# Conformer module of a decoder trunk: convolution taps on TensorE and VectorE, whole projections, a lag of two tiles

## The chip, the cores and the metric

The kernel runs on one core of one Trainium2 chip. A core has five engines with an instruction queue each: TensorE (PE, matrix products; the loading of weights is shown apart as PEld), VectorE (DVE), ScalarE (ACT), GpSimd (POOL) and SyncE (SP, which here issues most DMAs). Each works through its queue in order and waits on semaphores for the others. The metric is the device time of one execution in microseconds (us). Three runs of the kernel before took 1326.22, 1327.00 and 1327.53 us, median 1327.0.

## What is computed

The program is two layers of a decoder over 512 tokens of 1024 channels: a mixed state-space and attention layer, a gated MLP, a Conformer convolution module, a second gated MLP. The change touches the Conformer alone:

```python
def conformer_conv_module(h, pw1_w, pw1_b, dw_w, dw_b, ln_w, ln_b, pw2_w, pw2_b):
    u = h @ pw1_w + pw1_b                                    # 512 x 2048
    u = u[..., :CONV_CH] * jax.nn.sigmoid(u[..., CONV_CH:])  # gate, 512 x 1024
    u = causal_depthwise_conv(u, dw_w, dw_b)                 # 31 taps per channel
    u = jax.nn.silu(layer_norm(u, ln_w, ln_b))               # over the 1024 channels
    return u @ pw2_w + pw2_b
```

`h` is the RMS-normalised residual stream, and the result is added to that stream.

## The kernel before

Activations lie with channels on the 128 partitions and the 512 tokens along the free dimension, so the 1024 channels are eight tiles, 0 to 7. A product in full precision is made of three TensorE passes: each weight block of 128x1024 is split into a rounded high half (`wh`, a copy on ScalarE, line 862) and the rest (`wl`, a subtraction, line 866, on VectorE for blocks 0 to 15, on GpSimd from 16 on), and `gemm` (lines 136 to 138) multiplies high by high, high by low and low by high. Blocks 0 to 15 are the first projection, two for each tile (value and gate); blocks 16 to 23 are the last one.

For each tile the code does this, in an order written out by hand (`tc.manual_schedule`), which is each engine's order:

- `project`: two products into PSUM banks `mm` (three of them). VectorE scales them by the token norm (`scaled`, line 222, and line 942), ScalarE takes the sigmoid (line 944), VectorE writes the gated tile into `u` (line 946), which has 30 zero columns in front.
- The convolution needs 31 shifted products. TensorE takes taps in groups of four: `u` goes to DRAM (`du`, line 956) and comes back in four shifted copies (line 959, tile tag `u4`), so that the 128 partitions hold 32 channels times 4 taps. A group is four matmuls of 128x32 weights, one for each quarter of the channels (line 885), into a bank `pa` (two of them). The weights are diagonal blocks that `make_diag` builds (line 842, GpSimd).
- `CONV` divides the taps: tiles 0 to 5 have four groups (16 taps) on TensorE, seven taps as products on ScalarE (line 917) added by GpSimd (line 918), eight on VectorE as multiply-adds (line 903); the first of these takes the TensorE result in `pa` as its addend, for tiles 1 to 4. Tiles 6 and 7 have seven groups on TensorE and three taps on VectorE, all of it in halves of 256 tokens, and so are their projections and gates.
- `merge` adds GpSimd's part, `sums` keeps running sums over tiles of the values and their squares, for the layer norm. From tile 2 on a matmul with `neg` subtracts a token mean that was estimated from tile 0 (line 891).

At the end, for each half of the tokens: `tail_sums` (line 995, TensorE), `moments` (lines 1000 to 1006 with `rsqrt`, sixteen small VectorE instructions), `spread` (line 1012, TensorE), then for each tile `normalise` (lines 1017, 1018 on VectorE, 1020, 1023 on ScalarE), `residue` (line 1028, VectorE) and `outputs` (lines 1035 to 1037, twelve matmuls for the first four output tiles). The other four output tiles are whole products behind that.

A tile's work is spread over two turns of the loop: in turn j, blocks 2j and 2j+1 are projected, GpSimd convolves tile j−1, VectorE tile j−2, and TensorE tile j−1 at the end of the turn.

Of the kernel before, what the change touches and what calls it, by code (L numbers as in the profile page):

```python
# [52 lines left out]
CONV = [(4, 7)] * 6 + [(7, 0), (7, 0)]  # L53
H = T // 2
U4 = 284
FILL = 2
SPR = 6
# [3 lines left out]
def kernel(ctx: ExitStack, tc: tile.TileContext, x, w_in, w_dt, w_out,  # L61
# [33 lines left out]
    def pload(group, pool, queue=nc.scalar):  # L95
        a, b = PGROUP[group]
        ptiles[group] = pool.tile([P, b - a], F32, name=f"par_{group}")
        queue.dma_start(ptiles[group], par[:, a:b])
# [713 lines left out]
    def conformer(norm, nxt):  # L812
        ops = norm.ops
        pad, width = 30, 30 + T + 2
        blk = lambda c: slice(c * P, (c + 1) * P)
        stack = con("stack")
        quad = lambda c: slice(32 * c, 32 * c + 32)
        s1 = sbt("s1", 1)
        s2 = sbt("s2s", 1)
        krows = phase[0].tile([64, T], F32R, name="krows")  # L820
        neg = phase[0].tile([64, P], F32R, name="neg")
        negf = sbt("cv", 2)[0:64, 0:P]
# [4 lines left out]
        dup = sbt("xh", 1, shape=[P, NB, 64])  # L827
        G.memset(dup, 0.0)
        ubuf = [phase[0].tile([P, width], F32, name=f"u{i}") for i in range(4)]
        for u in ubuf:  # L830
            G.memset(u[:, 0:pad], 0.0)
            G.memset(u[:, pad + T :], 0.0)
        w = lambda j, k: prm("dww", j * 31 + k)
        win = lambda j, k: ubuf[j % 3][:, k : k + T]
        half = lambda q: slice(H * q, H * q + H)
        u4, cvp, y, yp, raws, halves, diag = {}, {}, {}, {}, {}, {}, {}

        def make_diag(j):
            n = CONV[j][0]
            t = (sbt("dg", 6) if j < 6 else sbt("dl", 2, 1024))[:, : n * P]  # L840
            t = t.rearrange("p (g c m) -> p g c m", c=4, m=32)
            G.tensor_tensor(t.rearrange("p g c m -> p (g c) m"), stack.unsqueeze(1).to_broadcast([P, 4 * n, 32]),
                            prm("dw4", j * 32, 4 * n).unsqueeze(2).to_broadcast([P, 4 * n, 32]), op=ALU.mult)
            diag[j] = t

        def taps(j):
            npe, npl = CONV[j]
            k0 = min(4 * npe, 31)
            return range(k0, k0 + npl), range(k0 + npl, 31)
# [5 lines left out]
        def split_hi(i):  # L855
            if i in (20, 21):
                t = sbt("u4", 2, 8 * U4, F32R)
                halves[i] = t[:, :RING], t[:, RING : 2 * RING]
            else:
                a, b, n = ("xh", "xl", 1) if i in (15, 19) else ("wh", "wl", 3)  # L860
                halves[i] = sbt(a, n, RING, F32R), sbt(b, n, RING, F32R)
            S.copy(halves[i][0], raws[i])  # L862

        def split_lo(i):
            wh, wl = halves[i]
            (V if i < 16 else G).tensor_tensor(wl, raws.pop(i), f32(wh), op=ALU.subtract)  # L866
            if i + 3 < 24:
                load(i + 3)

        def project(i, q=None):  # L870
            bank = bank_of("mm")
            if q is None:
                gemm(bank, halves.pop(i), ops, True, True)
            else:
                gemm(bank[:, :H], halves[i], [(a[:, half(q)], b[:, half(q)]) for a, b in ops], True, True)
            return bank

        def conv_pe(j, q=None):
            n, k0 = (T, 0) if q is None else (H, q)
            npe = CONV[j][0]  # L880
            cv = cvp[j, q] = bank_of("pa")
            for g in range(npe):
                for c in range(4):
                    src = u4[j][:, c] if q is None else u4[j][:, q, c]
                    TE.matmul(cv[quad(c), :n], diag[j][:, g, c, :], src[:, 4 * g : 4 * g + n],  # L885
                              start=g == 0, stop=g == npe - 1 and j < 2)
            if j == 2:
                shift[0] = bank_of("pb")
                TE.matmul(shift[0], neg, krows, start=True, stop=True)
            if j > 1:  # L890
                TE.matmul(cv[:, :n], neg, krows if q is None else krows[:, half(q)], start=False, stop=True)

        def conv_dve(j, part):
            ks = list(taps(j)[1])
            if part == 0:
                y[j] = sbt("g", 16)
            n = len(ks)
            a, b = (4 * n + 5) // 11, (8 * n + 5) // 11
            for k in (ks[:a], ks[a:b], ks[b:])[part]:
                if j in (0, 5) and k == ks[0]:  # L900
                    V.tensor_scalar(y[j], win(j, k), w(j, k), None, op0=ALU.mult)
                    continue
                V.scalar_tensor_tensor(y[j], win(j, k), w(j, k), cvp[j, None] if k == ks[0] else y[j],  # L903
                                       op0=ALU.mult, op1=ALU.add)

        def conv_pool(j, part):
            ks = list(taps(j)[0])
            n = len(ks)
            if part == 0:
                yp[j] = sbt("yp", 2)  # L910
            a, b = (2 * n + 3) // 7, (5 * n + 3) // 7
            for k in (ks[:a], ks[a:b], ks[b:])[part]:
                if k == ks[0]:
                    S.activation(yp[j], win(j, k), AF.Identity, scale=w(j, k), bias=prm("dwb", j))
                    continue
                pr = sbt("pr", 2)
# [402 lines left out]
```

## Time and profile before

| | us |
|---|---|
| median of three runs | 1327.0 |
| the profiled execution, its own time | 1328.7 |
| its span, first to last instruction | 1326.9 |
| TensorE busy | 1288.5 |
| VectorE busy | 884.8 |
| GpSimd busy | 226.8 |

The Conformer's first matmul starts 742.5 us into the span, its last one ends near 958.9. "Busy" counts an instruction from its start to its end; matmuls overlap, so TensorE's busy share says little of how fast it works, and the granted clock (PEclk, 1.00 is full) is read beside it. A wait is idle time ahead of an instruction, put down to what ended it. Readings of the profile give line numbers of the kernel before.

### The profile page before, as it was taken

To read this page: it belongs to the slowest core of one execution; us is meant where nothing else is said; L and a number is where in the kernel's file an instruction comes from. 1 tells how busy PE (TensorE), PEld (TensorE's weight loads), DVE (VectorE), ACT (ScalarE), POOL (GpSimd) and SP (SyncE) were. 2 spreads that over 40 slices of the span, in tenths; PEclk is the share of its full clock that TensorE was granted. 3 is DMA by queue.
4 is the path that set the end of the run, shared out by engine and by line. 5 is a ranking of instruction groups with operands and counts; after the bars stand their busy time and mean duration, and the time that the engine had idled before them with its cause. 6 is when DMAs were issued, how large, how long until landed. Compare 5 with 4: busy or idle time off the path is not lost.

```text
span 1326.9 us, 17068 instructions
## 1 busy us (share of the span) xinstructions
PE 1288.5 (97%) x6480; PEld 1037.3 (78%) x6480; DVE 884.8 (67%) x1442; ACT 541.0 (41%) x855; POOL 226.8 (17%) x264
## 2 busy tenths in 40 slices
PE   8999999999999999999999999778999999999998
PEld 6878877778888888888888866557888888888887
DVE  7986769984368777777323378897667777774221
ACT  5465547853244333333223343325533333332120
POOL 0032205630210000000001186662500000000000
PEclk9999999989999999999999999789999999999999
DMA  6311222112232333333332373532233333333331
GB/s 219 96 49 64 65 80 62 52 48 80 96 98 95 96 95 98 99 103 91 88 102 90 96 185 106 141 93 71 83 95 96 95 96 98 100 98 97 108 112 38
DMA packets 41554, 125.19 MB, mean 94 GB/s; under 512 B 4864, under 2 KB 7808, under 8 KB 41472
## 3 DMA queue, kind: packets, MB, share of 16 engines
q1 hardware_dynamic: 40752, 123.56, 30.4%
q8 instruction: 51, 0.84, 0.3%
q10 hardware_dynamic: 720, 0.55, 0.2%
q14 instruction: 31, 0.25, 0.1%
HBM read 119.73 MB, written 4.35 MB: 94 GB/s over the span
## 4 chain that ended last, share of the span: by engine, by line
PE 69%; DVE 8%; POOL 2%; issue 1%; ACT 1%; POOLq 0%; ACTq 0%; DVEq 0%
PE mm L136 21%; PE mm L137 21%; PE mm L138 21%; DVE g L903 3%; POOL yp L918 1%; DVE wl L866 1%; DVE g L976 1%; PE pa L885 1%; PE pc L696 1%; PE pa L137 1%; PE pa L138 1%; PE pa L136 1%; PE pb L687 0%; POOL g L922 0%; PE mm L1036 0%
## 5 line engine op out<-in xcount | busy, mean ns | idle before, releaser
L136 PE MATMUL mm<-xr,wh 128*128 128x512 f32 (+1 forms) x1136 | 442.0, 389 | 1.0 <-ACT wh L862 1.0
L138 PE MATMUL mm<-xr,wl 128*128 128x512 f32 (+1 forms) x1136 | 439.8, 387 | 2.7 <-DVE wl L866 2.7
L137 PE MATMUL mm<-xr,wh 128*128 128x512 f32 (+1 forms) x1136 | 439.7, 387 | 0.0
L120 ACT CAST wh<-wr 128x1024 fp32r<-128x1024 f32 (+1 forms) x178 | 183.6, 1032 | 463.8 <-PE mm L137 420.2
L121 DVE TENSOR_TENSOR wl<-wr,wh 128x1024 fp32r<-128x1024 f32 (+1 forms) x178 | 214.2, 1204 | 162.9 <-ACT wh L120 157.5
L136 PEld LDWEIGHTS mm<-xr,wh 128*128 128x128 f32 x1136 | 214.6, 189 | 45.9 <-issue 2.8
L138 PEld LDWEIGHTS mm<-xr,wl 128*128 128x128 f32 x1136 | 214.8, 189 | 45.3 <-DVE wl L866 2.9
L137 PEld LDWEIGHTS mm<-xr,wh 128*128 128x128 f32 x1136 | 214.7, 189 | 41.7 <-DVE xr L184 0.4
L137 PE MATMUL mm<-g,wh 128*128 128x512 f32 x368 | 145.0, 394 | 0.0
L222 DVE TENSOR_TENSOR cv<-mm,nrb 128x512 f32<-128x512 f32 x114 | 78.2, 689 | 95.3 <-PE mm L138 90.5
L138 PE MATMUL mm<-g,wl 128*128 128x512 f32 x352 | 138.7, 394 | 0.0
L136 PE MATMUL mm<-g,wh 128*128 128x512 f32 x352 | 138.7, 394 | 0.0
L217 DVE SCALAR_TENSOR_TENSOR ct<-cv,par_ffn,ct 128x510 f32<-128x510 f32 (+1 forms) x176 | 131.0, 747 | 3.5 <-issue 0.4
L194 POOL TENSOR_TENSOR nsum<-nsum,nsq 128x512 f32<-128x512 f32 x21 | 33.8, 1611 | 433.1 <-ACT nsq L193 433.1
L137 PEld LDWEIGHTS mm<-g,wh 128*128 128x128 f32 x368 | 68.8, 187 | 17.1
L138 PEld LDWEIGHTS mm<-g,wl 128*128 128x128 f32 x352 | 65.8, 187 | 16.3
L136 PEld LDWEIGHTS mm<-g,wh 128*128 128x128 f32 x352 | 65.8, 187 | 16.3
L214 ACT ACTIVATE ct<-cv,par_ffn 128x512 f32<-128x512 f32 x88 | 71.4, 814 | 3.2 <-DVE cv L222 3.0
L918 POOL TENSOR_TENSOR yp<-yp,pr 128x512 f32<-128x512 f32 x36 | 59.9, 1663 | 37.4 <-ACT pr L917 35.8
L795 ACT ACTIVATE th<-ct 128x512 f32<-128x512 f32 x44 | 27.8, 632 | 84.5 <-DVE ct L217 84.4
L903 DVE SCALAR_TENSOR_TENSOR g<-u,par_conf,g 128x512 f32<-128x512 f32 x42 | 56.1, 1336 | 1.1
L806 DVE TENSOR_TENSOR h<-h,mm 128x512 f32<-128x512 f32 x16 | 11.0, 688 | 59.1 <-PE mm L138 59.1
(350 smaller groups left out, 1511.8 us busy)
## 6 DMA issues: line engine op xcount, KB each, us to landing
wr<-w_up SPq DMA_DIRECT2D x88, 512.0 KB, 3.5
wr<-w_in SPq DMA_DIRECT2D x29, 512.0 KB, 3.5
wr<-w_dn SPq DMA_DIRECT2D x32, 448.0 KB, 3.3
wr<-pw SPq DMA_DIRECT2D x24, 512.0 KB, 3.6
wr<-w_out SPq DMA_DIRECT2D x16, 512.0 KB, 3.6
wr<-w_dn SPq DMA_DIRECT2D x16, 512.0 KB, 3.5
u<-du SPq DMA_DIRECT2D x24, 262.0 KB, 4.7
u<-du SPq DMA_DIRECT2D x16, 140.0 KB, 2.9
```

The costliest lines, as they stand in the source:

```text
L120: S.copy(wh[:, :n], raw[:, :n])
L121: V.tensor_tensor(wl[:, :n], raw[:, :n], f32(wh[:, :n]), op=ALU.subtract)
L136: TE.matmul(bank, wh[:, c], xh, start=first and i == 0, stop=False)
L137: TE.matmul(bank, wh[:, c], xl, start=False, stop=False)
L138: end = TE.matmul(bank, wl[:, c], xh, start=False, stop=last and i == n - 1)
L194: eng.tensor_tensor(self.sum, self.sum, sq, op=ALU.add)
L214: S.activation(t, v, AF.Identity, bias=bias, scale=w(taps - 1))
L217: V.scalar_tensor_tensor(t[:, s:], v[:, : T - s], w(k), t[:, s:], op0=ALU.mult, op1=ALU.add)
L222: V.tensor_tensor(v, bank, rb, op=ALU.mult)
L795: S.activation(sg, c, AF.Silu)
L903: V.scalar_tensor_tensor(y[j], win(j, k), w(j, k), cvp[j, None] if k == ks[0] else y[j], op0=ALU.mult, op1=ALU.add)
L918: G.tensor_tensor(yp[j], yp[j], pr, op=ALU.add)
```

## The change

The Conformer's function is written anew; nothing else in the program changes but the size of its parameter tile.

- Taps: `GROUPS_PE = [6] * 7 + [8]`. Tiles 0 to 6 have six groups (24 taps) on TensorE and the other seven on VectorE (`taps`); tile 7 has eight groups (32 taps, one of them zero) on TensorE, in two halves. GpSimd and ScalarE do no taps.
- `make_diag` is on VectorE, one tile in each turn. The windows `u4` have three buffers instead of two, `du` takes only the columns that are needed.
- All projections are whole. TensorE's convolution of tile j−2 stands in turn j between its two projections, VectorE's taps of tile j−1 in two parts, and TensorE's result is added once (`add`).
- `sums` are on VectorE for all tiles. Weight blocks 16 to 19 are split on VectorE. Blocks 20 to 22 are split behind the second half's normalisations.
- The sums, moments and spreads of the two halves stand close together at the end, the second moments between tiles 2 and 3 of the first half's normalisations.

```diff
-CONV = [(4, 7)] * 6 + [(7, 0), (7, 0)]
+GROUPS_PE = [6] * 7 + [8]
...
+        def make_diag(j):
+            n = GROUPS_PE[j]
+            t = sbt("dg", 4, RING)[:, : n * P].rearrange("p (g c m) -> p g c m", c=4, m=32)
+            V.tensor_tensor(t.rearrange("p g c m -> p (g c) m"), stack.unsqueeze(1).to_broadcast([P, 4 * n, 32]),
+                            prm("dw4", j * 32, 4 * n).unsqueeze(2).to_broadcast([P, 4 * n, 32]), op=ALU.mult)
+            diag[j] = t
...
+        def conv_pe(j, q=None, part=None):
+            n, t0 = (T, 0) if q is None else (H, H * q)
+            npe = GROUPS_PE[j]
+            if part in (None, 0):
+                cvp[j, q] = bank_of("pa")
+            cv = cvp[j, q]
+            gs = range(npe) if part is None else range(npe // 2 * part, npe // 2 * (part + 1))
+            for g in gs:
+                for c in range(4):
+                    TE.matmul(cv[quad(c), :n], diag[j][:, g, c, :], u4[j][:, c, 4 * g + t0 : 4 * g + t0 + n],
                               start=g == 0, stop=g == npe - 1 and j < 2)
...
+        def taps(j, part):
+            ks = list(range(4 * GROUPS_PE[j], 31))
             if part == 0:
                 y[j] = sbt("g", 16)
+            m = (len(ks) + 1) // 2
+            for k in (ks[:m], ks[m:])[part]:
                 if k == ks[0]:
+                    V.tensor_scalar(y[j], win(j, k), w(j, k), prm("dwb", j), op0=ALU.mult, op1=ALU.add)
+                else:
+                    V.scalar_tensor_tensor(y[j], win(j, k), w(j, k), y[j], op0=ALU.mult, op1=ALU.add)
+
+        def add(j):
+            V.tensor_tensor(y[j], cvp.pop((j, None)), y[j], op=ALU.add)
...
+        def evacuate(q):
             if q == 0:
+                y[7], sq[7] = sbt("g", 16), sbt("nsq", 1)
+            for dst, fn in ((y[7], AF.Identity), (sq[7], AF.Square)):
+                S.activation(dst[:, half(q)], cvp[7, q][:, :H], fn, bias=prm("dwb", 7))
...
+            for j in range(7):
                 pa = project(2 * j)
                 if j == 0:
                     norm.reduce()
+                split_w(2 * j + 2)
+                make_diag(j)
                 if j >= 1:
+                    taps(j - 1, 0)
                 if j > 0:
                     va = scaled(pa, norm.rb)
+                if j >= 2:
+                    conv_pe(j - 2)
+                if j == 3:
+                    shift_mean()
                 pg = project(2 * j + 1)
...
+                split_w(2 * j + 3)
                 if j >= 1:
+                    taps(j - 1, 1)
                 if j >= 2:
+                    add(j - 2)
...
+                if j >= 4:
+                    sums(j - 2)
                 gate(j, va, pg)
+            pa = project(14)
+            make_diag(7)
+            split_w(16)
+            taps(6, 0)
+            va = scaled(pa, norm.rb)
+            pg = project(15)
+            split_w(17)
+            taps(6, 1)
+            gate(7, va, pg)
             conv_pe(5)
+            split_w(18)
+            add(5)
             sums(5)
+            conv_pe(6)
+            split_w(19)
+            add(6)
+            sums(6)
+            conv_pe(7, 0, 0)
+            conv_pe(7, 0, 1)
+            evacuate(0)
+            conv_pe(7, 1, 0)
             bank = tail_sums(0)
             lr = moments(bank)
+            conv_pe(7, 1, 1)
+            evacuate(1)
...
+            sa = spread(lr)
+            bank = tail_sums(1)
...
             normalise(0, 0, sa)
+            for j in range(1, 8):
                 normalise(j, 0, sa)
                 residue(j - 1, 0)
+                if j == 2:
+                    lr = moments(bank)
+            residue(7, 0)
+            for j in range(8):
                 outputs(j, 0)
+                if j == 4:
+                    sa = spread(lr)
             for j in range(8):
+                normalise(j, 1, sa)
                 if j:
                     residue(j - 1, 1)
             residue(7, 1)
+            for i in (20, 21, 22):
+                split_w(i)
             for j in range(8):
                 outputs(j, 1)
+            split_w(23)
```

In the rows below, as the built programs hold them, a row is line, operation, output and inputs by the program's names, output shape; `x3` marks equal rows in a run. VectorE before, one turn of the loop (turn 4: `g` is a tile's convolution, `u` the gated tiles, `pa` TensorE's part, `cv` the scaled projections, `wl` a low weight half):

```order
L866 TENSOR_TENSOR wl_6976<-wr_6751,wh_6975 128x1024
L903 SCALAR_TENSOR_TENSOR g_6994<-u_6419,par_conf,pa_6930 128x512
L903 SCALAR_TENSOR_TENSOR g_6994<-u_6419,par_conf,g_6994 128x512 x2
L222 TENSOR_TENSOR cv_6998<-mm_6950,nrb_6532 128x512
L866 TENSOR_TENSOR wl_7026<-wr_6837,wh_7025 128x1024
L903 SCALAR_TENSOR_TENSOR g_6994<-u_6419,par_conf,g_6994 128x512 x3
L942 TENSOR_TENSOR cv_7043<-mm_7000,nrb_6532 128x512
L946 SCALAR_TENSOR_TENSOR u_6418<-cv_6998,par_conf,th_7045 128x512
L903 SCALAR_TENSOR_TENSOR g_6994<-u_6419,par_conf,g_6994 128x512 x2
```

VectorE after, turn 6 (`dg` the diagonal weights, `s` and `s2s` the running sums, `nsq` the squares):

```order
L850 TENSOR_TENSOR wl_7152<-wr_6979,wh_7151 128x1024
L862 TENSOR_TENSOR dg_7157<-ctile,par_conf 128x768
L904 TENSOR_SCALAR g_7159<-u_6419,par_conf 128x512
L906 SCALAR_TENSOR_TENSOR g_7159<-u_6419,par_conf,g_7159 128x512 x3
L221 TENSOR_TENSOR cv_7164<-mm_7126,nrb_6531 128x512
L850 TENSOR_TENSOR wl_7218<-wr_7038,wh_7217 128x1024
L906 SCALAR_TENSOR_TENSOR g_7159<-u_6419,par_conf,g_7159 128x512 x3
L909 TENSOR_TENSOR g_7042<-pa_7166,g_7042 128x512
L918 TENSOR_TENSOR s_1287_6406<-s_1287_6406,g_7042 128x512
L919 TENSOR_TENSOR s2s_6407<-s2s_6407,nsq_7227 128x512
L868 TENSOR_TENSOR cv_7231<-mm_7192,nrb_6531 128x512
L872 SCALAR_TENSOR_TENSOR u_6417<-cv_7164,par_conf,th_7233 128x512
```

Two taps less, the diagonal weights and two sums more; the convolution's own addition waits for a `pa` that TensorE finished one projection earlier, and no tap reads `pa`.

TensorE before, from the spread of the first half's moments on:

```order
L1012 MATMUL pb_7691<-ctile,lr_7619 128x128 x4
L885 MATMUL pa_7696<-u_1461_7294,dl_6925 32x256 x28
L891 MATMUL pa_7696<-krows,neg 128x256
L1035 MATMUL mm_7782<-dg_7732,wh_7563 128x256
L1036 MATMUL mm_7782<-g_7740,wh_7563 128x256
```

TensorE after, from the end of projection 15 on (`x24` are the six groups of a tile, `x32` the eight of half a tile):

```order
L889 MATMUL pa_7329<-u_1408_7119,dg_7040 32x512 x24
L895 MATMUL pa_7329<-krows,neg 128x512
L889 MATMUL pa_7366<-u_1425_7236,dg_7157 32x512 x24
L895 MATMUL pa_7366<-krows,neg 128x512
L889 MATMUL pa_7403<-u_1440_7322,dg_7268 32x256 x32
L895 MATMUL pa_7403<-krows,neg 128x256
L889 MATMUL pa_7441<-u_1440_7322,dg_7268 32x256 x16
L946 MATMUL pb_7458<-ones,s_1287_6406 128x1
```

Behind the last projection stand three tiles of convolution in a row, with no projection between or behind them, and the first half's sums stand in the middle of the last of these; before, half projections stood between the pieces.

More of the change, by code (lines that the diff above doesn't have):

```diff
@@ L96, in pload @@
         a, b = PGROUP[group]
-        ptiles[group] = pool.tile([P, b - a], F32, name=f"par_{group}")
+        room = 640 if group == "conf" else b - a
+        ptiles[group] = pool.tile([P, room], F32, name=f"par_{group}")[:, : b - a]
         queue.dma_start(ptiles[group], par[:, a:b])
@@ L826, in conformer @@
         V.tensor_copy(neg, negf)
-        dup = sbt("xh", 1, shape=[P, NB, 64])
+        dup = phase[0].tile([P, NB, P], F32, name="dup")
         G.memset(dup, 0.0)
-        ubuf = [phase[0].tile([P, width], F32, name=f"u{i}") for i in range(4)]
+        ubuf = [phase[0].tile([P, width], F32, name=f"u{i}") for i in range(3)]
         for u in ubuf:
             G.memset(u[:, 0:pad], 0.0)
-            G.memset(u[:, pad + T :], 0.0)
+            G.memset(u[:, pad + T : pad + T + 2], 0.0)
         w = lambda j, k: prm("dww", j * 31 + k)
         win = lambda j, k: ubuf[j % 3][:, k : k + T]
[L835 to L849, printed above, removed]
+        u4, cvp, y, sq, raws, halves, diag = {}, {}, {}, {}, {}, {}, {}
+        high, low, act = {}, {}, {}
         def load(i):
@@ L871, in project @@
             bank = bank_of("mm")
[L872 to L875, printed above, removed]
-            return bank
[L878 to L882, printed above, removed]
+            gemm(bank, halves.pop(i), ops, True, True)
@@ L886, in conv_pe @@
                               start=g == 0, stop=g == npe - 1 and j < 2)
             if j == 2:
[L888 to L894, printed above, removed]
+                cvp["shift"] = bank_of("pb")
+                TE.matmul(cvp["shift"], neg, krows, start=True, stop=True)
@@ L895, in conv_dve @@
+            if j > 1 and part in (None, 1):
+                TE.matmul(cv[:, :n], neg, krows[:, t0 : t0 + n], start=False, stop=True)
+        def taps(j, part):
+            ks = list(range(4 * GROUPS_PE[j], 31))
             if part == 0:
                 y[j] = sbt("g", 16)
[L897 to L904, printed above, removed]
@@ L978, in evacuate @@
[L978 to L986 removed]
+                t = sbt("nsq", 1)
+                S.activation(t, y[j], AF.Square)
@@ new lines, in sums, with shift_mean, shift_rows @@
+                V.tensor_tensor(s1, s1, y[j], op=ALU.add)
+                V.tensor_tensor(s2, s2, t, op=ALU.add)
+        def shift_mean():
+            bank = bank_of("pc")
+            tok_sum(bank, 0, y[0])
+            for o in (0, 32):
+                V.tensor_scalar(dup[:, :, o : o + 1], bank[:, :NB].unsqueeze(2), 1.0 / P, None, op0=ALU.mult)
+        def shift_rows():
+            bank = bank_of("pb")
+            for c in range(NB):
+                TE.transpose(bank[:, blk(c)], dup[:, c, :], ident)
+            S.copy(krows, bank)
+            V.tensor_tensor(krows[32:64], bank[32:64], f32(krows[32:64]), op=ALU.subtract)
```

252 lines of the change are left out of this document (43 added, 209 removed).

## The prediction

> **What bounds the kernel now.** The page comes first: which engine has no room, and where does it still have holes? The columns of the 40 slices are 33.2 us each.
>
> ```profile
> PE 1288.5 (97%) x6480; PEld 1037.3 (78%) x6480; DVE 884.8 (67%) x1442; ACT 541.0 (41%) x855; POOL 226.8 (17%) x264
> ...
> POOL 0032205630210000000001186662500000000000
> PEclk9999999989999999999999999789999999999999
> ```
>
> TensorE is the bound nearly everywhere. The one long dip of its granted clock (7 and 8, in the 26th and 27th slice) lies where GpSimd is busy (8, 6, 6, 6 from the 24th on): the Conformer, 742 to 958 us. So I ask what TensorE waits for there (us in total, times, longest):
>
> ```profile
> PE pa L885 <- DVE g L927: 6.6, 1, 6.6
> PE pa L885 <- DMA u<-du: 5.8, 1, 5.8
> PE mm L1035 <- ACT dg L1023: 4.6, 1, 4.6
> PE mm L138 <- DVE wl L866: 2.7, 1, 2.7
> PE pc L158 <- DVE g L924: 2.4, 1, 2.4
> PE pb L1012 <- DVE lr L153: 2.2, 2, 1.5
> PE mm L136 <- ACT wh L862: 1.0, 1, 1.0
> ```
>
> That is 25.3 us of idle TensorE. The stretches say what follows a wait (columns: stretch, its length, busy time and instructions of PE, PEld, DVE, ACT, POOL, granted clock, DMA share, GB/s):
>
> ```profile
> 760.96:771.85 10.89, 10.89 (x49) 8.82 (x47) 6.40 (x7) 8.35 (x13) 8.73 (x6) 1.00 0.85 242
> 742.50:771.85 29.35, 29.35 (x138) 24.32 (x136) 14.53 (x28) 15.22 (x21) 12.80 (x18) 1.00 0.48 133
> 771.85:775.50 3.65, 3.65 (x33) 0.94 (x32) 3.58 (x3) 1.64 (x2) 3.65 (x4) 1.00 0.55 171
> 781.10:784.75 3.65, 3.65 (x34) 0.95 (x33) 2.83 (x4) 0.93 (x2) 1.54 (x1) 1.00 0.20 79
> 792.90:812.00 19.10, 18.97 (x104) 13.38 (x105) 15.70 (x18) 7.80 (x12) 12.81 (x8) 1.00 0.41 108
> 842.20:860.20 18.00, 14.35 (x97) 13.84 (x96) 16.03 (x17) 5.42 (x8) 9.79 (x6) 0.81 0.51 132
> 904.40:909.30 4.90, 4.83 (x25) 4.49 (x25) 4.56 (x13) 4.27 (x9) 0.00 (x0) 0.65 0.25 102
> 742.50:936.65 194.15, 168.68 (x1177) 127.95 (x1176) 152.78 (x220) 81.65 (x123) 110.32 (x77) 0.94 0.41 111
> ```
>
> The first row is two whole projections: 5.45 each. The third and fourth are one convolution tile each (four groups, sixteen taps): 3.65, and the projection between them takes 781.10 − 775.50 = 5.60. Behind the 2.4 wait (it ends at 792.9) the clock stays 1.00; behind the 5.8 and the 4.6 wait it is 0.81 and 0.65. The stretch that the change rewrites, from the first projection to the last output of the second half, is the 194.15 us of the last row; the four matmul blocks behind it stay.
>
> Why does VectorE keep TensorE waiting at 67%? Line 903 is the same operation with two kinds of input (min/median/max ns):
>
> ```profile
> L903 DVE SCALAR_TENSOR_TENSOR g<-u,par_conf,g x42: 741/1634/1776, 772.9 to 877.0; 128x512 f32<-128x512 f32 x42
> L903 DVE SCALAR_TENSOR_TENSOR g<-u,par_conf,pa x4: 734/737/742, 794.1 to 852.2; 128x512 f32<-128x512 f32 x4
> ```
>
> With one input in PSUM (`pa`) it always takes 0.74; with both in SBUF it takes 0.74 or about 1.65, and GpSimd is at its own taps and sums while these run. I read the slow price as GpSimd's doing. The Trainium skill ("SBUF — State Buffer", "Who interferes with whom") says the same: a VectorE instruction with two SBUF inputs contends with a GpSimd instruction that reads SBUF, one with at most one SBUF input, outside the two-port modes, does not; these two rows agree.
>
> **The change part by part.** GpSimd's taps go, six groups (24 taps) of tiles 0 to 6 go to TensorE, the other seven stay on VectorE, tile 7 is all TensorE's. *VectorE per tile*, at prices without GpSimd:
>
> ```profile
> L222 DVE TENSOR_TENSOR cv<-mm,nrb 128x512 f32<-128x512 f32 x6 | 4.1, 681 | 3.6 <-ACT nrb L168 3.6
> L946 DVE SCALAR_TENSOR_TENSOR u<-cv,par_conf,th 128x512 f32<-128x512 f32 x6 | 4.7, 787 | 4.7 <-ACT th L944 4.7
> ...
> 792.75 1.22 DVE L866 TENSOR_TENSOR wl<-wr,wh 128x1024 fp32r<-128x1024 f32 x1
> ...
> 797.91 1.71 DVE L866 TENSOR_TENSOR wl<-wr,wh 128x1024 fp32r<-128x1024 f32 x1
> ...
> 813.28 0.69 DVE L936 TENSOR_TENSOR s<-s,g 128x512 f32<-128x512 f32 x1
> ...
> L842 POOL TENSOR_TENSOR dg<-ctile,par_conf 128x512 f32<-128x512 f32 x6 | 6.9, 1172 | 0.0
> ```
>
> Two weight halves 2.44, seven taps 5.18, two scalings 1.36, `u` 0.79 and 0.79 waiting for its sigmoid, three additions 2.07; and `make_diag`, which no row shows on VectorE: 128x768 lies between 0.92 (the 1.22 of a 128x1024 subtraction on the same engine, by size) and 1.76 (GpSimd's 1.17 for 128x512 of the same operation, by size); I take the former, since the engine is the same. Sum 13.6 us. *TensorE per tile*: two projections, six groups and the mean row, 5.45 + 5.60 + 5.37 + 0.32 = 16.7. So VectorE has 3 us to spare in each tile (14.4 by the dear end still fits; tile 4 also takes in the mean row and the sums of tiles 0 and 1, five additions and a copy, some 4 us, and hands about 1 on, which the next tile makes good), each weight half is split a whole projection ahead, and a tile's convolution comes two tiles behind its gate: the waits for L927, `u<-du`, `wl`, `wh` and L924 have no cause left until projection 15. What hides VectorE's and the DMAs' work is TensorE's own 16.7; gone it is only where no projection follows, at the end. ScalarE loses its products for GpSimd and gains nothing but two evacuations of tile 7. On SP's queue ten windows (two tiles came in halves) become eight, each 2 to 3% wider; they stand behind the same weight loads.
>
> *TensorE's sum, from the start to there.* A group costs 0.86 (3.65 less 0.2 of lead-in, by four), so a six-group tile 5.37. The start to projection 4 stays: 29.35. Projections 5 to 15: five behind a convolution (28.0), six not (32.7). Convolutions 0 to 4: 26.9. Four mean rows, the mean's sums (1.05) and transposes (0.6), small terms read off the timeline: 2.9. Together 119.9.
>
> *The end of the convolution.* Tile 7's window must come through DRAM before its convolution. Rows of tile 4 before, the write, the four reads and TensorE's start:
>
> ```profile
> 826.30 0.75 DVE L946 SCALAR_TENSOR_TENSOR u<-cv,par_conf,th 128x512 f32<-128x512 f32 x1 [0.79 <-ACT th L944]
> ...
> 827.08 0.33 SPq L956 DMA_DIRECT2D du<-u  x1
> ...
> 829.17 1.75 SPq L959 DMA_DIRECT2D u<-du  x4
> ...
> 836.38 5.46 PE L885 MATMUL pa<-u,dg 128*32 128x512 f32 x32 [5.80 <-DMA u<-du]
> ```
>
> That is 9.3 us from `u` to the matmul, with weight loads beside it. In the new order VectorE does gate 6 (2.3), `make_diag(7)` (1.2), a half, four taps, a scaling, a half and three taps (8.3 in all), 11.8 together, while TensorE does projections 14 and 15 (10.9); gate 7 (2.3) so ends 3.2 behind projection 15 and its window lands at 12.5. Convolutions 5 and 6 end at 11.2: a wait of 1.3, or 2.4 with `make_diag(7)` at its dear end, or none if the way through DRAM takes 8 us instead of 9.3. I take 0.8.
>
> ```profile
> 870.24 3.23 PE L885 MATMUL pa<-u,dl 128*32 128x256 f32 x56
> ...
> 888.82 0.28 PE L995 MATMUL pb<-ones,s 128*128 128x1 f32 x2
> ...
> 890.52 0.36 PE L136 MATMUL mm<-xr,xh 128*128 128x256 f32 x1
> ...
> 918.71 0.16 DVE L1003 SCALAR_TENSOR_TENSOR m<-mv,m 128x2 f32<-128x2 f32 x1
> ...
> 921.08 0.16 DVE L1006 SCALAR_TENSOR_TENSOR lr<-mv,lr 128x2 f32<-128x2 f32 x1
> ```
>
> A half tile of seven groups is 3.2, so eight groups 3.6 and 0.3 for the mean row; half of the second half 1.8; the sums 1.7 (888.82 to 890.52); the moments 2.9 (0.4 for two small instructions, 2.4 from L1003 to L1006, the last 0.16), of which the rest of the convolution (2.1) covers most; the spread 1.1. From projection 15: 11.2 + 0.8 + 3.9 + 1.8 + 1.7 + 3.0 + 1.1 = 23.5.
>
> *The outputs.*
>
> ```profile
> 902.36 0.41 DVE L1017 TENSOR_TENSOR g<-g,pb 128x256 f32<-128x256 f32 x1
> ...
> 904.38 0.43 DVE L1028 TENSOR_TENSOR g<-ct,dg 128x256 fp32r<-128x256 f32 x1 [0.37 <-ACT dg L1023]
> ...
> 904.40 0.39 PE L1035 MATMUL mm<-dg,wh 128*128 128x256 f32 x1 [4.58 <-ACT dg L1023]
> ...
> 917.50 0.28 PE L1035 MATMUL mm<-dg,wh 128*128 128x256 f32 x1
> ...
> 918.93 0.28 PE L1035 MATMUL mm<-dg,wh 128*128 128x256 f32 x1
> ```
>
> From VectorE's first normalisation to the first output are 2.0 us; one tile's twelve matmuls take 1.43 (917.50 to 918.93), VectorE's three operations 1.2. The second half's sums on TensorE (1.7) cover all but 0.3 of the 2.0. But the second moments now stand on VectorE ahead of tile 3: three normalisations and two residues 3.5, moments 2.9, normalisation 3 0.8, residue 2 0.35, so tile 2 has its low half 7.55 behind the spread, and TensorE has done tiles 0 and 1 by 2.0 + 0.5 + 2 × 1.43 = 5.4. A **new wait of 2.2**; behind the moments are queued normalisations 3 to 7, which at 1.2 a tile then keep ahead of TensorE's 1.43. First pass 17.5 (2.0, the residue's 0.5, eight tiles 11.4, the wait 2.2, the second spread 1.1, edges), second pass 8 × 1.43 = 11.5. Sum 29.0. Casts 20 to 22 now stand behind the second pass on ScalarE, but end 1.5 us ahead of their use.
>
> Sum: 119.9 + 23.5 + 29.0 = 172.4 for what took 194.15, so **−21.8 us**. A ledger of differences says nearly the same: waits −25.3; slow clock −8.7 (18.0 for 11.4 of work and 3.7 of waits, 4.9 for 2.9, a convolution 5.46 for 3.64, and 2.0 taken for the one behind the 6.6 wait); four projections whole instead of in halves −1.1 (48 × 0.119 against 5.45 each); twelve more groups (50 for 38) +10.3; new waits +4.5: −20.1. The profiled execution took 1328.7 (span 1326.9 and 1.8 around it), giving 1307; the median of the runs shown is 1327.0, 1.7 less, so I say 1306, between the two sums.
>
> **The rivals.** *A late window.* Should the reads of tile 7 take 3 us more (a weight load is issued right behind them), TensorE idles 3.8 us and starts tile 7 at the low clock, which cost 2 to 4 us behind the waits above: 1306 + 3 + 3 = 1312. For it: the 5.8 wait and the 5.46 behind it. Against: the 9.3 was itself measured with such loads beside it. The Trainium skill ("TensorE: Matmul & The Clock Gate", "What's actually happening") puts the loss of clock at an idle window of about 3.4 us. By that rule the forecast's waits, none over 2.2, cost only themselves, and a window late by 3 us costs the clock too; the rows behind the 2.4 and the 4.6 wait agree.
>
> *VectorE's taps stay slow*, GpSimd being innocent: 13.6 + 7 × 0.9 = 19.9 a tile against 16.7; tiles 2 to 6 lose 3.2 each: 1322. The change would then still gain, by the waits at the end alone. Against it: all four `pa` rows at 0.74.
>
> *Slower than before*: every two-input operation stays at its dear price (halves 1.71, taps 1.65, `make_diag` 1.76, sums about 1.7). VectorE's tile is then 23.8, it sets TensorE's pace through the wait for `wl` in tiles 1 to 6, and 6 × 7.1 = 43 more turns −21.8 into +21: 1349. It decides from 20.3 us a tile on (21.8 / 6 above 16.7). Against it: 1.22 and 0.69 stand in the rows above, in moments when GpSimd rests.
>
> *The end costs less*: the window is on time and residue 2 does not stop TensorE: −3 to −5, 1302.
>
> **How the numbers follow.** The forecast, 1302 to 1310, has 0.68; the late window (1310 to 1315) 0.13; the cheaper end (1299 to 1302) 0.07; slow taps 0.06; slower than before 0.03; the change giving back all it gains, by a wait that I do not see, 0.03. The range that leaves two in ten out takes the forecast, most of the late window and part of the cheaper end: 1300 to 1314. Faster by over 0.2% (about what a measurement of this kernel can tell from no change) 0.95, within it 0.02, slower 0.03.
>
> **What would show it.** Right: the taps' median at 0.74; in TensorE's waits nothing over 1 us between the start and convolution 6; granted clock 0.99 there; then waits of about 1 (window), 1 (moments) and 2 (residue 2). Wrong: a wait for `wl` or `u<-du` in mid tile (VectorE or the queue is late), a clock below 0.9 at tile 7 (late window), or a convolution tile above 5.6.

## The result, and the profile after

The changed kernel takes 1305.97 us (median of four runs, 1305.71 to 1309.42) against 1327.26 us (median of four, 1326.22 to 1328.27) on the same chip: ratio 0.9849, 95% interval 0.9834 to 0.9864, so 1.5% less time. The profiled execution took 1305.71 us, its span is 1303.9. Of all the executions below, one, of the kernel with five groups in tiles 0 and 2, fell into a slow state, 2131.56 us at a mean clock of 0.56 where its other four took 1300.96 to 1302.20, and it is left out of its ratio. Lines are from here on those of the changed kernel, unless another is named.

First the page: busy times, and the rows of 40 slices for GpSimd and for TensorE's granted clock.

```profile
PE 1287.4 (99%) x6431; PEld 1028.8 (79%) x6431; DVE 855.6 (66%) x1444; ACT 514.3 (39%) x812; POOL 123.3 (9%) x198
...
POOL 0032204630210000000000100000500000000000
PEclk9999999999999999999999999999999999999999
```

GpSimd is idle in the Conformer (slices 24 to 28; its last weight halves come in the 29th), and the dip in the clock's row is gone. TensorE's busy time has hardly changed (1288.5 before): what went is idle time and slow work. The waits of TensorE from 700 to 960 us, seven rows and 25.3 us before, are now (us in total, times, longest):

```profile
PE pa L889 <- DMA u<-du: 2.6, 1, 2.6
PE pb L963 <- DVE lr L152: 0.6, 1, 0.6
PE mm L989 <- DVE g L981: 0.4, 1, 0.4
PE mm L988 <- ACT dg L978: 0.4, 1, 0.4
```

All four lie behind the last projection. VectorE's taps, in the view of one line (min/median/max ns), and two other groups of its instructions by line and shape (count, busy us, mean ns):

```profile
L906 DVE SCALAR_TENSOR_TENSOR g<-u,par_conf,g x42: 745/752/754, 759.5 to 857.7; 128x512 f32<-128x512 f32 x42
```

```profile
L850 DVE TENSOR_TENSOR wl<-wr,wh 128x1024 fp32r<-128x1024 f32 x17 | 20.8, 1221 | 1.6 <-ACT wh L849 1.6
...
L862 DVE TENSOR_TENSOR dg<-ctile,par_conf 128x768 f32<-128x768 f32 x7 | 6.7, 952 | 0.0
```

The median tap fell from 1634 to 752 ns, and not one of the 42 is slow. A weight half takes 1.22 on average, the diagonals 0.95.

How much of the 23 us between the two profiled spans did the Conformer gain? The norm's sum on TensorE stands right behind the first projection of the Conformer, and again in the MLP behind it, so from one to the other is a fair stretch to compare. Timeline before, then after:

```profile
748.21 0.95 PE L158 MATMUL pb<-ones,nsum 128*128 128x1 f32 x8
964.16 0.95 PE L158 MATMUL pb<-ones,nsum 128*128 128x1 f32 x8
```

```profile
744.26 0.95 PE L157 MATMUL pb<-ones,nsum 128*128 128x1 f32 x8
941.06 0.95 PE L157 MATMUL pb<-ones,nsum 128*128 128x1 f32 x8
```

215.95 us became 196.80: 19.15 less. The other 3.95 us were gained ahead of it, in code that the change does not touch. One stretch there shows most of it; the row before, then after (stretch, length, busy us and instructions of PE, PEld, DVE, ACT, POOL, granted clock, DMA share, GB/s):

```profile
290.00:305.00 15.00, 15.00 (x63) 12.20 (x62) 8.52 (x24) 4.18 (x7) 0.00 (x0) 0.77 0.21 69
```

```profile
290.00:305.00 15.00, 15.00 (x71) 12.09 (x72) 11.56 (x28) 7.00 (x11) 0.00 (x0) 1.00 0.21 71
```

At a clock of 0.77 instead of 1.00, 15 us do the work of 11.6. Whether that belongs to the change is the first question for the experiments. The second is where the rest of the forecast gain stayed: the stretches of the changed kernel's Conformer, from the norm's sum on.

```profile
744.26:857.86 113.60, 113.60 (x633) 78.11 (x632) 87.29 (x127) 25.48 (x30) 0.00 (x0) 1.00 0.54 147
857.86:872.00 14.14, 11.51 (x100) 3.32 (x99) 8.52 (x11) 3.85 (x5) 0.00 (x0) 0.98 0.86 225
872.00:877.39 5.39, 5.39 (x69) 2.86 (x73) 0.00 (x0) 0.00 (x0) 0.00 (x0) 0.73 0.26 103
877.39:885.11 7.72, 7.08 (x93) 5.01 (x92) 2.47 (x16) 2.58 (x5) 0.00 (x0) 1.00 0.01 2
885.11:913.74 28.63, 27.70 (x216) 27.18 (x216) 21.58 (x66) 20.80 (x38) 3.46 (x2) 0.94 0.01 2
888.50:892.00 3.50, 3.50 (x19) 3.50 (x18) 3.02 (x19) 1.08 (x2) 0.00 (x0) 0.51 0.00 0
```

Up to the end of projection 15 (first row) TensorE never stops and has the full clock. Then come convolutions 5 and 6 and the wait for the last window, the first half of tile 7 at a clock of 0.73, the rest to the spread, and the outputs, with a spell at 0.51 in them (last row, a part of the one above).

The last window's own way, on VectorE's and on SP's queue:

```profile
859.89 0.75 DVE L872 SCALAR_TENSOR_TENSOR u<-cv,par_conf,th 128x512 f32<-128x512 f32 x1 [0.85 <-ACT th L870]
```

```profile
855.02 1.56 SPq L839 DMA_DIRECT2D wr<-pw  x2
860.68 0.33 SPq L876 DMA_DIRECT2D du<-u  x1
864.09 1.75 SPq L878 DMA_DIRECT2D u<-du  x4
865.94 1.68 SPq L839 DMA_DIRECT2D wr<-pw  x2
```

From the end of `u` (860.64) to the matmul (872.00) are 11.4 us, with two weight loads issued ahead of the write and two behind the reads. The forecast had taken 9.3.

### The profile page after: what moved, and what is told of

The parts are those of the page before. It is cut to its first block, busy times and chain, and to the rows that moved or that the text cites. A ratio compares the mean times of both kernels' runs of the same rounds, so it can differ in the third digit from the quotient of the medians.

```text
span 1303.9 us, 16808 instructions
## 1 busy us (share of the span) xinstructions
PE 1287.4 (99%) x6431; PEld 1028.8 (79%) x6431; DVE 855.6 (66%) x1444; ACT 514.3 (39%) x812; POOL 123.3 (9%) x198
## 4 chain that ended last, share of the span: by engine, by line
PE 77%; DVE 3%; DMA 1%; issue 1%; POOL 0%; ACT 0%; SPq 0%; ACTq 0%; POOLq 0%
PE mm L135 23%; PE mm L137 23%; PE mm L136 23%; PE pa L889 3%; PE pc L695 1%; PE pa L135 1%; PE pa L137 1%; PE pa L136 1%; PE pb L686 1%; DMA u<-du 0%; PE mm L989 0%; PE mm L990 0%; PE mm L988 0%; PE pb L163 0%; POOL lt L670 0%
## 5 line engine op out<-in xcount | busy, mean ns | idle before, releaser
L135 PE MATMUL mm<-xr,wh 128*128 128x512 f32 x1120 | 439.5, 392 | 0.0
L136 PE MATMUL mm<-xr,wh 128*128 128x512 f32 x1120 | 437.5, 391 | 0.0
L137 PE MATMUL mm<-xr,wl 128*128 128x512 f32 x1120 | 437.5, 391 | 0.0
L137 PEld LDWEIGHTS mm<-xr,wl 128*128 128x128 f32 x1120 | 210.4, 188 | 43.9 <-issue 0.2
L135 PEld LDWEIGHTS mm<-xr,wh 128*128 128x128 f32 x1120 | 210.7, 188 | 43.6 <-issue 1.6
L136 PEld LDWEIGHTS mm<-xr,wh 128*128 128x128 f32 x1120 | 210.7, 188 | 43.2 <-DVE xr L183 0.4
L136 PE MATMUL mm<-g,wh 128*128 128x512 f32 x360 | 141.8, 394 | 0.0
L135 PE MATMUL mm<-g,wh 128*128 128x512 f32 x352 | 138.7, 394 | 0.0
L889 PE MATMUL pa<-u,dg 128*32 128x512 f32 (+1 forms) x464 | 46.4, 550 | 2.6 <-DMA u<-du 2.6
L889 PEld LDWEIGHTS pa<-u,dg 128*32 128x32 f32 x464 | 14.7, 114 | 29.4 <-issue 23.0
```

What stands on the lines that cost most here:

```text
L135: TE.matmul(bank, wh[:, c], xh, start=first and i == 0, stop=False)
L136: TE.matmul(bank, wh[:, c], xl, start=False, stop=False)
L137: end = TE.matmul(bank, wl[:, c], xh, start=False, stop=last and i == n - 1)
L889: TE.matmul(cv[quad(c), :n], diag[j][:, g, c, :], u4[j][:, c, 4 * g + t0 : 4 * g + t0 + n], start=g == 0, stop=g == npe - 1 and j < 2)
```

## The experiments

In them the two theories are these. **Contention**: GpSimd's additions made VectorE's taps slow, VectorE kept TensorE waiting, and the gain is the end of that. **Order**: the lag of two tiles, the whole projections and the new places of the work took the waits away. All times in "norm sum to norm sum" are read as above, and leave out what happens ahead of the Conformer. The runs come from three chips, on which the kernel before had medians of 1327.93 to 1328.23 us.

### The changed kernel once more

No edit.

> The changed kernel once more, unaltered. Its profile ran the unchanged code ahead of the Conformer 3.95 us earlier than the profile of before (norm-sum matmul at 744.26 against 748.21), and the granted clock at 290 to 305 us was 1.00 against 0.77. Theory: this low clock comes and goes between executions of the same code, so about one in five to one in two of these runs lies 3 to 4 us above the lowest, and the median stays at 1305.5 to 1306.5. Rival: the clock spell belongs to the kernel before alone (code or buffers of the Conformer shift something ahead of it); then all runs here agree within 1 us, and all of the kernel before lie within 1 us too.

1307.81 us (1307.42 to 1308.02, four runs); before 1327.95 (eight runs); ratio 0.9852, 0.9838 to 0.9867. The stretch with the slow clock, and the norm's sum:

```profile
290.00:305.00 15.00, 15.00 (x61) 12.17 (x60) 8.16 (x23) 4.65 (x7) 0.00 (x0) 0.78 0.19 70
```

```profile
747.73 0.95 PE L157 MATMUL pb<-ones,nsum 128*128 128x1 f32 x8
```

The same program now shows the clock of before, and reaches the norm's sum 3.47 us later. So the spell comes and goes between executions, and does not belong to the change. The expected median (1305.5 to 1306.5) was missed: the spell was there in the profiled run, and the other three runs took as long as that one. The Conformer, though, took less than in the first profile, 195.03 us (the next norm sum starts at 942.76). The difference is the last window:

```profile
861.33:875.13 13.80, 11.52 (x99) 3.32 (x99) 8.51 (x11) 3.85 (x5) 0.00 (x0) 1.00 0.86 226
875.13:879.11 3.98, 3.98 (x69) 2.62 (x73) 0.00 (x0) 0.00 (x0) 0.00 (x0) 1.00 0.43 169
```

A wait of 2.29 us instead of 2.63, and behind it the full clock: 3.98 us for what took 5.39. In this one run the view of the waits puts the wait down to VectorE's last sum, which ended 0.1 us before the matmul. With the split window further on, the same matmul starts 1.6 us ahead of that sum (869.88 and 871.43), so it does not depend on it, and the wait counts here as one for the window. These 195.03 us are the yardstick below.

### GpSimd made busy again

```diff
+        idle = phase[0].tile([P, T], F32, name="idle")
+        G.memset(idle, 0.0)
...
+                G.tensor_tensor(idle, idle, win(j, k), op=ALU.add)
```

> The changed kernel with an idle GpSimd made busy: beside each of the 49 taps on VectorE, GpSimd adds the tap's window into a tile that nothing reads. Output unchanged. Theory (GpSimd's SBUF traffic makes VectorE's taps slow): the taps' median goes from 0.75 to between 1.2 and 1.7 us, VectorE's tile from 13.6 to 17 to 20 us, TensorE waits in tiles 2 to 6 again, 2 to 16 us in all: 1308 to 1322. Rival (the gain came from the new order and the lag of two tiles, and the slow taps of before from something else): taps stay at 0.75 and the time within 2 us of the changed kernel.

1332.34 us (1330.19 to 1334.38), ratio 1.0036 (1.0023 to 1.0050): all of the gain is gone. The taps, and TensorE's waits:

```profile
L909 DVE SCALAR_TENSOR_TENSOR g<-u,par_conf,g x42: 740/1462/1673, 764.3 to 884.8; 128x512 f32<-128x512 f32 x42
```

```profile
PE pa L889 <- DMA u<-du: 15.0, 2, 9.4
PE pb L934 <- DVE dup L929: 6.0, 1, 6.0
PE mm L993 <- DVE g L985: 1.9, 1, 1.9
```

The taps are slow as before, with the new order in place. Contention is right in kind; the size (1308 to 1322) was too small, because VectorE's other operations suffer as well:

```profile
L850 DVE TENSOR_TENSOR wl<-wr,wh 128x1024 fp32r<-128x1024 f32 x17 | 27.1, 1592 | 1.3 <-ACT wh L849 0.8
...
L862 DVE TENSOR_TENSOR dg<-ctile,par_conf 128x768 f32<-128x768 f32 x7 | 12.6, 1801 | 0.0
...
L907 DVE TENSOR_SCALAR g<-u,par_conf 128x512 f32<-128x512 f32 x7 | 9.2, 1311 | 0.0
...
L913 DVE TENSOR_TENSOR g<-pa,g 128x512 f32<-128x512 f32 x7 | 4.8, 683 | 0.0
```

The diagonals go from 0.95 to 1.80, the weight halves from 1.22 to 1.59; the last row, with one input in PSUM, stays at 0.68. This run is also the rival "slower than before" come true, on a smaller scale.

### Before, without GpSimd's additions

```diff
-                G.tensor_tensor(yp[j], yp[j], pr, op=ALU.add)
...
-                G.tensor_tensor(y[j], y[j], yp.pop(j), op=ALU.add)
```

> The kernel before without GpSimd's additions of its taps and without the addition of their sum to VectorE's: GpSimd's share of the taps of tiles 0 to 5 is missing from the output. Order, lag, windows, half projections and ScalarE's products stay. Theory (contention, not order, makes VectorE late): VectorE's slow taps fall from about 1.65 to 0.75 us, the waits of 6.6, 5.8 and 2.4 us and the slow clock behind them go: 12 to 18 us less than before. Rival (the order and the lag of one tile cause the waits): under 5 us less.

1304.13 us (1302.68 to 1304.65), ratio 0.9819 (0.9803 to 0.9834): 24 us less than before, more than expected. VectorE's taps are the same 42 instructions in the same order as before:

```profile
L903 DVE SCALAR_TENSOR_TENSOR g<-u,par_conf,g x42: 736/752/2137, 773.2 to 853.5; 128x512 f32<-128x512 f32 x42
```

```profile
PE mm L1033 <- ACT dg L1021: 4.6, 1, 4.6
PE pb L1010 <- DVE lr L153: 2.3, 2, 1.5
PE pb L164 <- DVE nr L153: 1.2, 1, 1.2
```

Median 752 instead of 1634, and the waits of 6.6, 5.8, 2.7 and 2.4 us are gone, with order and lag untouched. ScalarE's products stay in this run, so they did not make the taps slow. The wait of 2.4 us is no proof of contention, though: before, VectorE stood idle for 4.5 us ahead of it until GpSimd's own addition of line 922 was done, and that addition is left out here too. The 4.6 us at the first output stay: they belong to the order.

### The new division in the old order

The run before this one leaves work out, so its time is no version's. Here the changed kernel's division (six groups, seven taps, none on GpSimd) stands in the old order.

```diff
-CONV = [(4, 7)] * 6 + [(7, 0), (7, 0)]
+CONV = [(6, 0)] * 6 + [(7, 0), (7, 0)]
...
-            if j < 5:
-                G.tensor_tensor(y[j], y[j], yp.pop(j), op=ALU.add)
...
+            V.tensor_tensor(y[j], y[j], cvp[j, None], op=ALU.add)
```

> The kernel before with the changed kernel's division of the taps and with nothing else of the change: six groups on TensorE and seven taps on VectorE in tiles 0 to 5, no taps on GpSimd or ScalarE, the bias with VectorE's first tap; order, lag of one tile, half projections and GpSimd's diagonals and sums as before. Nothing is left out. From the run without GpSimd's additions (1304.1) twelve more groups cost 12 x 0.86 = 10.3. Theory (the division alone brings most of the gain, by ending the contention; order, lag and whole projections bring the rest, some 6 to 8 us): 1312 to 1316. Rival (the division is all there is): 1306 to 1309. Rival (without the new order the longer convolution runs into windows that are late): 1318 or more.

1310.91 us (1309.73 to 1314.20), ratio 0.9877 (0.9862 to 0.9893), a little under the expected 1312 to 1316. From norm sum to norm sum it is 200.56 us (744.86 to 945.42): the division alone takes 15.4 off the 215.95, and order, lag, whole projections and VectorE's sums another 5.5 (to 195.03). Where those 5.5 are is seen in the waits that are left:

```profile
PE mm L1030 <- ACT dg L1018: 4.6, 1, 4.6
PE pb L1007 <- DVE lr L153: 2.0, 2, 1.3
```

6.6 us, both in the outputs of the old order, against 1.5 there and 2.3 at the last window in the changed kernel (the second profile): 2.8 of the 5.5. The half projections are 1.1 by the prediction's price. The rest, some 1.6, fits the slow clock behind the 4.6 wait: from 886.12 to 889.64 the granted clock is 0.52, which costs 3.52 × 0.48 = 1.7 us by estimate. No run tested this split.

### Seven groups, and five

```diff
-GROUPS_PE = [6] * 7 + [8]
+GROUPS_PE = [7] * 7 + [8]
```

> Seven groups of taps on TensorE in tiles 0 to 6 instead of six, so three taps each on VectorE instead of seven. Theory (TensorE sets the pace, a group costs 0.86 us): seven more groups cost 6.0 us, less 0 to 2 that VectorE's shorter queue gives at the last window: 1310 to 1312. Rival (VectorE or the windows still set the pace somewhere): less than 3 us more, or a gain.

1309.03 us (1307.55 to 1311.32), below the expected 1310 to 1312. From norm sum to norm sum 198.59, which is 3.56 more than the yardstick. The sum comes out: seven groups at 0.86 cost 6.0, and the wait of 2.29 is gone (the last two convolutions are longer, and VectorE has fewer taps ahead of the last gate). The whole time, 1.2 more, would have met the rival's figure; the stretch meets the theory's, both in the price of a group and in what a late group covers.

```diff
-GROUPS_PE = [6] * 7 + [8]
+GROUPS_PE = [5] * 7 + [8]
```

> Five groups on TensorE in tiles 0 to 6, so eleven taps each on VectorE. By the prediction's prices TensorE's tile is 16.7 - 0.86 = 15.85 and VectorE's 13.6 + 3.0 = 16.6. Theory: VectorE becomes the bound by a little: TensorE saves 6.0, waits of 1 to 5 us appear in tiles 4 to 6 and the last window comes 2 to 4 us later: 1303 to 1309. Rival (TensorE alone sets the pace, VectorE has more room than the sum says): the full 6.0 are gained, 1300. Third: the waits bring the low clock with them, 1310 or more.

1314.82 us (1312.15 to 1316.55), the third case. TensorE gains 4.5 us up to projection 15, and then pays for it:

```profile
PE pa L889 <- DMA u<-du: 12.9, 2, 6.5
```

```profile
880.27:886.03 5.76, 5.76 (x65) 2.99 (x65) 0.00 (x0) 0.00 (x0) 0.00 (x0) 0.63 0.24 95
```

VectorE, now with 11 taps a tile, has no pause from 840 to 869 us in its timeline but 0.85 us for each sigmoid; it brings the windows of tiles 6 and 7 too late, and the first half of tile 7 (the row above) then runs at a clock of 0.63. With six groups it had room: 12.81 us busy, and 0.85 waiting for a sigmoid, in the 16.66 from convolution 3 to convolution 4.

### The last window

Three edits: the gate ahead of a weight half and three taps; the three loads beside the window issued from ScalarE's queue, behind the evacuation of the first half; both.

```diff
             pg = project(15)
+            gate(7, va, pg)
             split_w(17)
             taps(6, 1)
-            gate(7, va, pg)
```

> The changed kernel with the last tile's gate (three VectorE instructions that write its window) moved ahead of the weight half and the three taps that stood in front of it on VectorE. Theory: the window is written 0.5 to 1 us earlier, so the wait of 2.3 to 2.6 us becomes 1.5 to 2 and the clock stays 1.00 behind it: 1 to 2.5 us less than the changed kernel. Rival (the way through DRAM sets the time, and VectorE is not what is late): within 0.5 us of it.

```diff
-            if i + 3 < 24:
+            if i + 3 < 24 and i not in (17, 18, 19):
...
             evacuate(0)
+            for i in (20, 21, 22):
+                load(i, nc.scalar)
```

> The changed kernel with the three weight loads that share the queue and the time of the last window's write and reads issued from ScalarE's queue instead, behind the evacuation of the first half tile. Theory (the loads beside it slow the window's transfer): write to reads falls from 3.5 to about 2.1 us, reads to matmul from 7.5 to 5 to 6, the wait goes, 2.3 to 4 us less than the changed kernel. Rival (the way through DRAM takes this long by itself): wait unchanged, within 0.5 us; or the late loads turn into a wait of TensorE in the matmul blocks behind, 1 us or more above it.

> Both edits of the two runs before this one: early gate and moved loads. Theory: no wait for the last window is left, 2.5 to 4 us less than the changed kernel, about 1304 where that takes 1307. Rival: the wait moves to the moments or the outputs, less than 1 us gained.

| | whole time, median | norm sum to norm sum | wait for the last window |
|---|---|---|---|
| changed kernel, once more | 1307.81 | 195.03 | 2.3 |
| early gate | 1306.70 | 193.82 | 1.1 |
| moved loads | 1306.49 | 193.97 | 1.2 |
| both | 1305.00 | 193.91 | 1.2 |

By the stretch each alone takes some 1.1 us off, and both together no more: the wait did not go. The whole time of the third run says 2.8, but its four runs lie in two pairs, 1303.4 and 1303.6, 1306.4 and 1306.6, three microseconds apart as the slow stretch ahead of the Conformer is. The first two are in part as expected: with the loads moved, the write takes 2.4 us instead of 3.5 (start of the write to start of the reads),

```profile
864.19 0.34 SPq L876 DMA_DIRECT2D du<-u  x1
866.60 1.74 SPq L878 DMA_DIRECT2D u<-du  x4
```

but from the reads to the matmul (874.09) it is still 7.5 us, with no load beside them. The loads were thus not what made the reads slow. With both edits, the rows of the stretches show where most of that time goes:

```profile
867.00:869.00 2.00, 2.00 (x21) 0.68 (x24) 2.00 (x3) 0.00 (x0) 0.00 (x0) 1.00 0.71 176
869.00:871.00 2.00, 2.00 (x24) 0.52 (x16) 1.72 (x4) 1.57 (x2) 0.00 (x0) 1.00 1.05 214
871.00:873.00 2.00, 1.91 (x17) 0.45 (x9) 1.10 (x2) 0.00 (x0) 0.00 (x0) 1.00 0.86 161
873.00:875.00 2.00, 0.91 (x20) 0.70 (x24) 1.93 (x3) 0.63 (x1) 0.00 (x0) 1.00 0.01 2
```

The DMA engines are full with the window's own 1.06 MB (four reads of 266 KB), at some 210 GB/s, which makes 5 of the 7.5 us. The last 1.1, from 873.0 to the matmul at 874.09, pass with the DMA engines at rest (0.01); no run takes them apart.

Why does the early gate gain nothing on top of the moved loads? SP's queue with the early gate alone tells most of it:

```profile
859.35 0.37 SPq L839 DMA_DIRECT2D wr<-pw  x1
...
868.62 4.29 SPq L839 DMA_DIRECT2D wr<-pw  x3
```

The moved gate also stands ahead of `split_w(17)`, which issues a weight load. So this edit, too, takes one of the two loads from ahead of the window's write and puts it behind the reads, and the write takes 2.4 us here as well (864.35 to 866.78). VectorE itself starts `u` only 0.39 us earlier (1.65 us behind the start of convolution 5 instead of 2.04), where 0.5 to 1 was expected. The two edits thus share their main effect. With both, the write takes 2.8 us, and the load issued at 859 is still under way beside it; why just these 0.4 us are lost again is not settled.

### A window in two parts

If the bytes set the time, the first half tile need not wait for all of them.

```diff
-            for s in range(4):
-                nc.sync.dma_start(u4[j][quad(s), :, 0:n], ...)
+            for a, b in ((0, 284), (284, n)) if j == 7 else ((0, n),):
+                for s in range(4):
+                    nc.sync.dma_start(u4[j][quad(s), :, a:b], ...)
```

> Early gate and moved loads, and the last window's reads in two sets of four, first the columns of the first half tile, then the rest. With whole reads 1.06 MB takes 5 us at 212 GB/s. Theory (the reads take their time by their bytes): the first half lands some 2.4 us earlier, the wait of 1.2 us goes, 1.0 to 1.3 us less in the Conformer (193.9 us from norm sum to norm sum becomes 192.7) and 1303 to 1304 in all. Rival (eight reads instead of four cost as much in issuing and in latency as they save): within 0.5 us.

1302.38 us (1301.75 to 1305.63), ratio 0.9819 (0.9803 to 0.9834); norm sum to norm sum 192.84, where 192.7 was expected. The DMA view (KB each, median us to landing) of the two parts:

```profile
u<-du SPq DMA_DIRECT2D x4, 142.0 KB, 3.0
...
u<-du SPq DMA_DIRECT2D x4, 128.0 KB, 3.7
```

TensorE's only wait that the view still lists is the 0.6 for the moments. Now the end has room, and VectorE can take groups back where it has room too:

```diff
-GROUPS_PE = [6] * 7 + [8]
+GROUPS_PE = [5, 6, 5, 6, 6, 6, 6, 8]
```

> The run with the split window, and five groups instead of six on TensorE in tiles 0 and 2. Theory (VectorE has 3 us to spare in a tile, a five-group tile takes 3.9 of it, the six-group tile behind makes it good): TensorE saves 2 x 0.86 = 1.7 us, no new wait: 191.0 us from norm sum to norm sum. Rival (tile 4's additions already use up the room): a wait of 1 us or more in tiles 3 to 6, or a late last window, and no gain or a loss of up to 3 us.

1301.67 us, ratio 0.9803 (0.9789 to 0.9816); norm sum to norm sum 190.91, where 191.0 was expected, and no wait over 0.64. With a third five, in tile 4:

> As the run with five groups in tiles 0 and 2, and tile 4 has five as well. Theory (VectorE still has room): 0.86 us less again, 190.05 us from norm sum to norm sum. Rival (the room is used up in tile 5, which takes in tile 4's four more taps on top of the additions left over from tile 4's turn): the last window is late by 1 us or more, and nothing is gained or 1 to 2 us are lost, 191 to 193.

1302.59 us (1298.96 to 1303.01), ratio 0.9804 (0.9790 to 0.9818); norm sum to norm sum 190.02, where 190.05 was expected. The whole times of these two cannot be told apart: ahead of the Conformer the clock moves them by more than the 0.9 us between them. Both beat the changed kernel and the kernel before.

## Why the prediction was right, and where it was not

**Contention** is shown from both sides: GpSimd busy beside the new order gives the slow taps and the old time back, and the old order without GpSimd's additions gives fast taps and 24 us less. What is shown is that GpSimd's work slows VectorE's; by what path, no run tests. The Trainium skill ("SBUF — State Buffer", "Who interferes with whom") was cited for it. The trace agrees: an addition with one input in PSUM stayed at 0.68. A TENSOR_SCALAR with its one large input in SBUF went from 0.54 to 1.31; the page excepts such an operation only outside the two-port modes, and whether this one runs in them no trace here shows. VectorE's tile was put at 13.6 us with 0.79 of waiting for a sigmoid in it; from convolution 3 to 4 (819.10 to 835.76) VectorE is busy for 12.81 and waits 0.85 for one, 13.66 together (a tile has one tap less than before, seven for eight in the rows ahead of the prediction, not two). The diagonals, taken at 0.92 between 0.92 and 1.76, took 0.95. The five-group run confirms the bound: VectorE falls behind where, by its expectation, 16.6 stands against 15.85.

**TensorE's sum to projection 15** was 119.9. The stretch from the norm's sum is 113.60, and 5.71 lie ahead of it (742.50 to 748.21 before): 119.3. A tile of six groups took 5.36 (forecast 5.37):

```profile
767.99 5.36 PE L889 MATMUL pa<-u,dg 128*32 128x512 f32 x48
```

The signs named for this part came: no wait, a clock of 1.00, the median tap at 0.75.

**The end of the convolution** is the term that was mis-sized: 23.5 forecast, 27.25 measured (857.86 to 885.11). Convolutions 5 and 6 took 11.51 (11.2), and the rest behind tile 7's first half 7.72 (7.6). The window's wait was 2.63, not 0.8, and the clock then cost 1.41 (5.39 against 3.98). The cause is the way through DRAM: 11.4 us, not the 9.3 that one row of tile 4 before had shown. From the write to the reads were 3.4 us (2.1 in that row), from the reads to the matmul 7.9 (7.2). The runs split the excess: the loads beside it make the write about 1.1 us longer, and the reads take 7.5 us with no load beside them, in 5 of which the DMA engines are full with the window's own bytes. The upper bound of 2.4 for this wait came from VectorE's diagonals alone; the DRAM way had been given a lower bound (8 us), but no upper one. That case stood among the rivals as the late window (6 us more), and it came in part: the sign that the prediction gave for it, a clock below 0.9 at tile 7, is there in the first profile (0.73) and not in the second (1.00).

**The outputs**: 29.0 forecast, 28.63 measured. The **new wait** of 2.2 for the moments ahead of tile 3 showed as 0.4 only, so that one could think it wrong; in its place are 3.5 us at a clock of 0.51. The last run has the other form, its wait and the stretch from the first output to that wait's end:

```profile
PE mm L990 <- DVE g L982: 1.9, 1, 1.9
```

```profile
882.87:888.40 5.53, 3.52 (x25) 3.12 (x25) 5.01 (x24) 2.31 (x5) 0.00 (x0) 1.00 0.01 1
```

At the full clock the wait is 1.94, and from the end of the spread to the next norm sum both take the same: 55.95 (885.11 to 941.06) and 55.96 (880.78 to 936.74). In both, tile 2's low half is used 7.62 us behind the spread (892.73 and 888.40), where the prediction had 7.55. VectorE sets this moment; whether TensorE gets there slowly or waits is all one.

**The sum** was −21.8 (the ledger beside it adds up to −20.3, not −20.1). The three parts measure 119.3 + 27.25 + 28.63 = 175.2 instead of 172.4, so the Conformer gained 19.0 of the 194.15 in the first profile and 20.9 (215.95 − 195.03) in the second. That the whole time still came out at 1305.97 for 1306 is in part luck, with the clock ahead of the Conformer: there the profiled execution before was slow and the one after was not, worth the 3.95 us, and no part of the prediction. With the slow stretch in it the changed kernel takes 1307.8. The 1.7 us between the profiled execution and the median before, which the prediction named without a cause, are of that size.

## What to carry to other kernels

An engine that is not the bound can still set the pace by slowing its neighbour: where one operation shows two durations in a single run, look for the engine that is active in the slow cases, and price the plan at the fast duration once that engine is idle. Price a transfer at the end of a phase by its bytes, by the idle time around them and by what shares the DMA engines with it, not by one latency read elsewhere, give its price an upper bound as well as a lower one, and let the first consumer start on a part of it. When engines are close to balance, divide the work tile by tile, and compare stretches of the program, from mark to mark, where the whole time wanders by more than the step under test.

## What the runs showed of the hardware that was not expected

- The granted clock from 290 to 305 us, in code that is the same in all kernels here, was 0.77 or 0.78 (before, and the changed kernel once more), 0.89 (the last run), or 1.00 (the changed kernel's first profile, the run with the split window), and the Conformer's norm sum started between 744.3 us (at 1.00) and 748.3 us (at 0.77). What sets it stays open.
- After an idle time of 2.29 us TensorE went on at 1.00, after 2.63 us at 0.73. The Trainium skill ("TensorE: Matmul & The Clock Gate", "What's actually happening") puts the loss at an idle window of about 3.4 us, by which neither should have cost anything; the measurement decides. And 3.5 us at 0.51 came in the outputs, where the waits just before were 0.6 and 0.4 us, with sums of one column each between them. No run took these sums away, so their part in it is open.
